# An encoder layer on one core: the mixing's output projection with all eight feature tiles by seven block products, in two sets

## The chip, the core and the metric

The kernel runs on one core of a Trainium2 chip. Time is device time in microseconds of one launch. The core has five engines with queues of their own: TensorE (PE), VectorE (DVE), ScalarE (ACT), GpSimd (POOL) and SyncE (SP). SP and POOL also issue most of the DMAs. Each engine works through its queue in order, and engines wait for each other on semaphores.

## What is computed

One encoder layer over 512 tokens with 1024 channels, in float32: a half-step feed-forward, a mixing of two attention branches, and a second half-step feed-forward, each with an RMS norm ahead and behind.

```python
f = _swiglu(_rmsnorm(x, ffn1_pre_g[l]), ffn1_w_gate[l], ffn1_w_up[l], ffn1_w_down[l])
x = x + 0.5 * _rmsnorm(f, ffn1_post_g[l])
h = _rmsnorm(x, mix_pre_g[l])
proj = h @ w_in[l]
...
ya = _neighbourhood_attention(...) @ w_branch_a[l]
yb = _dilated_mixture(qb, kb, vb, slopes) @ w_branch_b[l]
merged = jax.nn.sigmoid(gate_a) * ya + jax.nn.sigmoid(gate_b) * yb
x = x + _rmsnorm(merged @ w_out[l], mix_post_g[l])
f = _swiglu(_rmsnorm(x, ffn2_pre_g[l]), ffn2_w_gate[l], ffn2_w_up[l], ffn2_w_down[l])
x = x + 0.5 * _rmsnorm(f, ffn2_post_g[l])
```

The change is in `merged @ w_out`: 512 tokens, 1024 features in, 1024 out.

## The kernel before

**Precision.** Each float32 operand is split into a high part (rounded to fp32r, a copy by ScalarE) and a low part (what is left, a subtraction by VectorE), in `split`, lines 110 and 111. A product is three matmuls, high with high, high with low and low with high, in `mm3`, lines 189 to 191.

**Block products.** Much of the kernel multiplies 2 x 2 blocks by seven products in place of eight. In the output projection the tokens are in halves, the outputs in halves, and the features in pairs of tiles that make up the two halves of a set. The class `Blocks` holds this. A product number i (1 to 7) takes a token operand and a weight operand. Some are blocks and some are sums of blocks: `tokens` makes the token sums on VectorE (lines 615 and 620), the weight sums `t1` to `t4` are made by DMAs that add into SBUF (issued by POOL), and one, `t2`, by VectorE in `rows`. `prep` splits both operands of one product. `run` does its 12 matmuls: two row tiles of 128 tokens, two features, three matmuls each. The results add up in pairs of PSUM banks: `q` (products 1, 4, 6, 7), `r` (product 2), `c` (5 and 3) and, before the change, `z`. `onto` moves one pair onto another: ScalarE copies the bank to SBUF (`part`, line 672), VectorE adds it (line 678).

**The stage.** A loop over eight tiles f makes `merged`, tile by tile: 30 matmuls each, two gated products and a sum on VectorE (lines 1303 to 1313). Tiles 0 to 3 become the operands of the seven block products, and tiles 4 to 7 are kept as `hidden` and multiplied in the ordinary way by `one`, with four weight pieces of their own. The list `order` says in which order operands are prepared, `seq` in which order the first seven steps run. Beside these, `by_dma` loads the first four weight pieces of the second feed-forward: POOL issues the high loads (line 136), ScalarE writes the negated copy (line 139), and POOL issues a load that adds the original to it (line 141).

**The end of the stage.** `rows_out` walks over the four row tiles t (row 0 to row 3, 128 tokens each) and over the last steps of each. When a half of a row is complete, ScalarE takes its sum of squares (`junk`, line 248) and VectorE multiplies it by the gain (line 435). When both are, POOL makes the reciprocal root (lines 256 to 260) and VectorE the new `x` (line 475), whose squares ScalarE takes again. `pre_norm` then makes the normalised row (line 268), TensorE transposes it (line 277), and ScalarE and VectorE copy it out as `hn` (lines 280 and 281). Here `turn` says behind which step of row t the row before is normalised and the one before that is transposed. The second feed-forward begins in `first_pairs` with row tiles 0 and 1, at line 203, and does the transposes of rows 2 and 3 between its first products.

**What sets the order.** A scheduler orders the instructions by a timeline of its own, except where the kernel pins them: from `ordered.append([mark()])` on to the first products of the feed-forward, PE, ACT and DVE keep the order of the program text. POOL keeps it from `way_out` on, and SP through the first feed-forward. The pool `wp` has room for six split weight pieces of 128 x 1024, high and low, and the next split waits until the product that used the oldest has run. The pool `hp` has four rooms, `ra` to `rd`, of two raw pieces each.

Of the kernel before, what the change touches and what calls it, by code (L numbers as in the profile page):

```python
# [13 lines left out]
F32R = mybir.dt.float32r  # L14
BF16 = mybir.dt.bfloat16
AF = mybir.ActivationFunctionType
ALU = mybir.AluOpType
# [3 lines left out]
P = 128  # L21
T = 512
D = 1024
NK = D // P
# [6 lines left out]
NPIECE = 6  # L31
SPREAD = 4
URGENT = 400
FIRST = (4, 5, 6, 7)
STD = 3
BLOCKS = (10, 10)
BYDMA = (2, 3, 4)
# [6 lines left out]
def block_kernel(ctx, tc, x, gains, weights, rpb_near, rpb_all, alibi0, alibi12, out):  # L44
    nc = tc.nc
# [12 lines left out]
    def unit(dt=F32, name="u"):  # L58
        return up.tile([P, 512], dt, tag="u", name=name)
# [6 lines left out]
    def bank(name="ps"):  # L66
        return pp.tile([P, 512], F32, tag="ps", name=name)
# [33 lines left out]
    def gain(i):  # L101
        g = gp.tile([P, D], F32, tag="gain", name=f"gain{i}")
        nc.sync.dma_start(g, gains[i:i + 1, :].partition_broadcast(P))
        return g
# [4 lines left out]
    def split(hi, lo, src):  # L109
        nc.scalar.copy(hi, src)  # L110
        nc.vector.tensor_tensor(lo, src, hi.bitcast(F32), op=ALU.subtract)  # L111


    pieces = {}
# [47 lines left out]
    def cut(w, c, n):  # L162

        return [a[c // 512][:, c % 512:c % 512 + n] for a in w]

    def take(ahead=True):
        w = pieces.pop(state["take"])
        state["take"] += 1
        if ahead:
            fill(NPIECE - 1)  # L170
        return w
# [16 lines left out]
    def mm3(o, sh, sl, mh, ml, start, stop, **kw):  # L188
        nc.tensor.matmul(o, sh, mh, start=start, stop=False, **kw)  # L189
        nc.tensor.matmul(o, sh, ml, start=False, stop=False, **kw)  # L190
        nc.tensor.matmul(o, sl, mh, start=False, stop=stop, **kw)  # L191
# [364 lines left out]
    class Blocks:  # L556
# [38 lines left out]
            self.raw[key] = to  # L595
            nc.sync.dma_start(to, block(*kind, d))

        def load_sum(self, key, at, *of):

            to = self.raw[key, 0] = self.duo_room(*at)  # L600
            nc.sync.dma_start(to, self.block(*of[0], 0))
            for b in of[1:]:
                yield
                nc.gpsimd.dma_start(to, self.block(*b, 0), accum_op=ALU.add)
            yield

        def tokens(self, i, d):

# [479 lines left out]
    def mixing(g):  # L1088
# [106 lines left out]
        g_post, g_pre = gain(g), gain(g + 1)  # L1195
# [19 lines left out]
        seq = [(g, h) for g in (1, 2, 0) for h in range(4)]  # L1215
# [20 lines left out]
        step(len(pend))  # L1236


        hidden = [None] * 8
        parts = {}  # L1240
        duos = [[None] * 2 for _ in range(2)]
        n0 = total - 3 * NF - NK
        o = Blocks(n0, 1, duos)
        sub, add = ALU.subtract, ALU.add
        b00, b01, b10, b11 = (0, 0), (0, 1), (1, 0), (1, 1)
        sums = []
        way_out = mark()

        def stat(k):
            if k not in parts:  # L1250
                parts[k] = unit(F32R), unit(F32R)
                split(*parts[k], hidden[k])
                hidden[k] = None
            return parts[k]

        def load_rows(n):
            if n == 0:
                sums.extend([o.load_sum(b10, ("ra", 0), b10), o.load_sum(b00, ("ra", 1), b00),
                             o.load_sum("t1", ("rb", 0), b00, b01), o.load_sum("t2", ("rb", 1), b00, b01, b11),
                             o.load_sum("t3", ("rc", 0), b11, b01), o.load_sum(b11, ("rc", 1), b11),  # L1260
                             o.load_sum("t4", ("rd", 0), b00, b01, b11, b10)])
            for l in sums:
                next(l, None)

        wt = {}
        rooms = deque()

        def one(acc, t, k, first=False):

            w = wt[k]  # L1270
            for i in range(2):
                hh, hl = stat(k[0] + i)
                ts = slice(t * P, (t + 1) * P)
                mm3(acc, hh[:, ts], hl[:, ts], *cut(w, i * 512, 512), first and i == 0, i == 1, skip_group_check=True)

        order = [(2, 0), (1, 0), ("z", 4, 1), (5, 0), (6, 0), ("r", 4, 0), (7, 0), (3, 0), ("w", 6, 0), ("w", 6, 1), (4, 0)]
        seq = order[:7]
        ready = []

        def prep(n):  # L1280
            while len(ready) <= min(n, len(order) - 1):
                s = order[len(ready)]
                ready.append(s)
                if len(s) == 2:
                    o.prep(*s)
                else:
                    for i in range(2):
                        stat(s[1] + i)
                    i = n0 + 4 + len(wt)
                    convert(i, rooms.popleft() if rooms else None)  # L1290
                    wt[s[1:]] = pieces.pop(i)

        br = {}
        for f in range(8):
            ya, yb = bank(), bank()
            for k in range(10):
                i, c = divmod((f * 10 + k) * P, PIECE)
                if i not in br:
                    br[i] = take()
                mm3(ya if k < 4 else yb, *cut(br[i], c, P), o_parts[k][0], o_parts[k][1],  # L1300
                    k in (0, 4), k in (3, 9))
            m1, m2 = unit(), unit()
            nc.vector.tensor_tensor(m1, ya, sig[f], op=ALU.mult)
            nc.vector.tensor_tensor(m2, yb, sig[8 + f], op=ALU.mult)
            if f < 4:
                for i in range(2):
                    if f % 2 == 0:
                        duos[i][f // 2] = unit(name="h")
                    part = slice(i * 256, i * 256 + 256)
                    nc.vector.tensor_tensor(duos[i][f // 2][:, (f % 2) * 256:(f % 2) * 256 + 256],  # L1310
                                            m1[:, part], m2[:, part], op=ALU.add)
            else:
                nc.vector.tensor_tensor(m1, m1, m2, op=ALU.add)
                hidden[f] = m1
                stat(f)
            if 1 <= f <= 4:
                load_rows(f - 1)
            if f == 4:
                rooms.append(o.duo_room("rd", 1))
                nc.sync.dma_start(rooms[-1], weights[n0 + 4])  # L1320
            if f in FIRST:
                prep(FIRST.index(f))
                if f > 4:
                    o.prep_tokens(f, 0)
                    rooms.append(o.duo_room("ra", f - 5) if f < 7 else o.duo_room("rb", 0))
                    nc.sync.dma_start(rooms[-1], weights[n0 + f])
        state["take"] = state["next"] = n0 + 8
        state["stop"] = total - 3 * NF + 2 * STD

        whole[:] = [[unit(name="whole") for _ in range(2)] for _ in range(2)]  # L1330
        early = [by_dma(n) for n in first_of_next()] * 2
        ordered.append([mark()])
        after = {(1, 0): ("r", "q", add), (5, 0): ("z", "c", add), (6, 0): ("c", "q", sub), (7, 0): ("z", "q", sub)}
        for n, s in enumerate(seq):
            if len(s) == 2:
                o.run(*s)
            else:
                for key in s[0]:
                    first = o.open(key)
                    for t in range(2):  # L1340
                        one(o.acc[key][t], t + 2 * (key in "qz"), s[1:], first)
            if s in after:
                o.onto(*after[s])
            prep(n + len(FIRST))
            for _ in range((2, 2, 1, 1, 1, 1, 0)[n]):
                next(early.pop(0))
        state["used"] = True
        state["next"] += SPREAD
        acc = o.acc["r"] + o.acc["q"], o.acc["c"] + o.acc["z"]
        tail = [((6, 0), (4, 1), (6, 1), "b")] * 2 + [((6, 1), (4, 0), (6, 0), "b")] * 2  # L1350

        def last(t, k):
            k = tail[t][k]
            if k == "b":
                o.run(4 if t > 1 else 3, 0, (t % 2,))
            else:
                one(acc[k[1]][t], t, k)

        rows_out(acc, range(4), (None, 0, 1, 1), last, lambda t, b: (0, 3, 3, 0)[b + 2 * (t > 1)], g_post, 1.0, g_pre, False, None, False)
        pool.append((way_out, mark(), (mybir.EngineType.Pool,)))  # L1360


# [39 lines left out]
    g_pre = [bank("gain"), bank("gain")]  # L1402
# [81 lines left out]
    for n0, n1, engines in [(*o, PINNED) for o in ordered] + [(0, state["sp"], (mybir.EngineType.SP,)), *pool]:  # L1484
        last = {}
# [58 lines left out]

def _out_pieces(w):

    n = len(w) // 2
    rest = _moving_pieces(w[n:])
    return np.concatenate([_moving_pieces(w[:n]), rest[[2, 0, 1, 3]]])


def _down_pieces(w, blocks):
# [52 lines left out]
```

## Time and profile before

| | us |
|---|---|
| median of 3 runs | 1090.49 |
| the runs | 1091.98, 1090.48, 1090.49 |
| the profiled execution | 1090.01 |
| its span | 1088.2 |
| output projection: first matmul to the first of the second feed-forward | 704.83 to 748.03 |

The span is the time between the first and the last instruction on the engines; the rest of the execution lies around it. A row of a timeline gives start and duration in us, the engine, the line, the operation, the tile written and the tiles read, the shape, how many were merged (x2), and in brackets the idle time ahead of it with what ended it. A tile name without its number stands for all its buffers. A matmul's duration in the profile is its passage through the pipeline; what it takes of TensorE is the distance between starts.

### The profile page before, as it was taken

How to read it: one execution, taken by the hardware profiler on the slowest of the kernel's cores; microseconds unless marked ns; L12 is line 12 of the kernel's file. 1: busy time of each engine (PE TensorE's matmuls, PEld its weight loads, DVE VectorE, ACT ScalarE, POOL GpSimd, SP SyncE). 2: the span in 40 equal slices, each digit the busy share in tenths (PEclk: the TensorE clock that was granted, in tenths of full speed). 3: DMA queues.
4: the chain of work that ended last, by engine and by line, in shares of the span. 5: the costliest groups of instructions: out<-in, count | busy, mean ns of one | idle time of the engine just before them, and what ended most of it. 6: DMA issues, size and time to landing. Idle time of an engine off the chain costs nothing. (4 is left out here: it accounts for less than half of the span.)

```text
span 1088.2 us, 18567 instructions
## 1 busy us (share of the span) xinstructions
PE 1078.8 (99%) x6821; PEld 977.7 (90%) x6821; DVE 819.7 (75%) x1514; ACT 649.3 (60%) x1300; POOL 177.9 (16%) x248
## 2 busy tenths in 40 slices
PE   9999999999999999999999999999999999999997
PEld 7999999998888988888988888888999999998886
DVE  7887777777987679876467654766897777779974
ACT  6555555565584767767656651375565555566662
POOL 3121122012334000000000001133131111114101
PEclk9999999999999999999999999999999999999999
DMA  6899898468994453332232239564577776769932
GB/s 215 223 200 241 217 244 207 138 164 252 233 296 101 126 183 119 135 90 79 66 104 78 78 118 300 162 116 140 140 188 206 196 170 182 200 174 248 237 139 77
DMA packets 90973, 184.59 MB, mean 170 GB/s; under 512 B 23553, under 2 KB 26113, under 8 KB 90882
## 3 DMA queue, kind: packets, MB, share of 16 engines
q1 hardware_dynamic: 64720, 131.03, 35.8%
q0 software_dynamic: 23472, 51.91, 26.8%
q8 instruction: 53, 0.87, 0.3%
q10 hardware_dynamic: 2690, 0.46, 0.2%
q14 instruction: 38, 0.31, 0.1%
HBM read 178.34 MB, written 7.58 MB: 171 GB/s over the span
## 5 line engine op out<-in xcount | busy, mean ns | idle before, releaser
L111 DVE TENSOR_TENSOR w<-raw,w 128x512 fp32r<-128x512 f32 (+1 forms) x139 | 129.3, 931 | 87.6 <-ACT w L110 87.0
L189 PE MATMUL ps<-hn,w 128*128 128x512 f32 (+1 forms) x488 | 174.9, 358 | 0.0
L110 ACT CAST w<-raw 128x512 fp32r<-128x512 f32 (+1 forms) x139 | 113.5, 819 | 102.5 <-DMA raw<-in_weights_dram 41.5
L191 PE MATMUL ps<-hn,w 128*128 128x512 f32 (+1 forms) x488 | 172.4, 353 | 0.0
L190 PE MATMUL ps<-hn,w 128*128 128x512 f32 (+1 forms) x488 | 172.3, 353 | 0.0
L110 ACT CAST w<-t 128x512 fp32r<-128x512 f32 x152 | 93.5, 619 | 52.0 <-DVE t L334 27.9
L111 DVE TENSOR_TENSOR w<-t,w 128x512 fp32r<-128x512 f32 x152 | 103.9, 688 | 27.1 <-ACT w L110 24.4
L191 PEld LDWEIGHTS ps<-hn,w 128*128 128x128 f32 x488 | 92.3, 189 | 12.9
L190 PEld LDWEIGHTS ps<-hn,w 128*128 128x128 f32 x488 | 92.4, 189 | 11.3
L189 PEld LDWEIGHTS ps<-hn,w 128*128 128x128 f32 x488 | 92.4, 189 | 11.3
L189 PE MATMUL q<-v,w 128*128 128x256 f32 x304 | 86.0, 283 | 0.0
L191 PE MATMUL q<-hn,w 128*128 128x256 f32 x304 | 86.0, 283 | 0.0
L189 PE MATMUL p<-v,w 128*128 128x256 f32 x304 | 86.0, 283 | 0.0
L190 PE MATMUL p<-v,w 128*128 128x256 f32 x304 | 86.0, 283 | 0.0
L191 PE MATMUL q<-v,w 128*128 128x256 f32 x304 | 86.0, 283 | 0.0
L190 PE MATMUL q<-v,w 128*128 128x256 f32 x304 | 86.0, 283 | 0.0
L190 PE MATMUL q<-hn,w 128*128 128x256 f32 x304 | 86.0, 283 | 0.0
L189 PE MATMUL q<-hn,w 128*128 128x256 f32 x304 | 86.0, 283 | 0.0
L191 PE MATMUL p<-v,w 128*128 128x256 f32 x304 | 85.9, 283 | 0.0
L328 POOL DMA_DIRECT2D t<-in_weights_dram x38 | 33.3, 877 | 289.5 <-DMA t<-in_weights_dram 67.3
L189 PE MATMUL q<-w,a 128*128 128x512 f32 x176 | 68.5, 390 | 0.0
L190 PE MATMUL q<-w,a 128*128 128x512 f32 x176 | 68.3, 389 | 0.0
(260 smaller groups left out, 2992.6 us busy)
## 6 DMA issues: line engine op xcount, KB each, us to landing
raw<-in_weights_dram SPq DMA_DIRECT2D x103, 512.0 KB
t<-in_weights_dram SPq DMA_DIRECT2D x76, 256.0 KB
t<-in_weights_dram POOLq DMA_DIRECT2D x76, 256.0 KB, 5.3
w<-in_weights_dram SPq DMA_DIRECT2D x38, 256.0 KB
w<-in_weights_dram POOLq DMA_DIRECT2D x36, 256.0 KB, 6.3
rows<-in_weights_dram SPq DMA_DIRECT2D x24, 256.0 KB
tb<-in_weights_dram POOLq DMA_DIRECT2D x12, 512.0 KB, 7.9
x<-in_x_dram SPq DMA_DIRECT2D x16, 256.0 KB
```

What stands on the lines that cost most here:

```text
L110: nc.scalar.copy(hi, src)
L111: nc.vector.tensor_tensor(lo, src, hi.bitcast(F32), op=ALU.subtract)
L189: nc.tensor.matmul(o, sh, mh, start=start, stop=False, **kw)
L190: nc.tensor.matmul(o, sh, ml, start=False, stop=False, **kw)
L191: nc.tensor.matmul(o, sl, mh, start=False, stop=stop, **kw)
L328: nc.gpsimd.dma_start(t1, weights[n][:, :512], accum_op=ALU.add)
```

## The change

All eight tiles of `merged` become operands of seven block products, in two sets d = 0 and 1 (tiles are taken in the pairs 0, 2, 1, 3 of `TURNS`, and the matrix is laid out accordingly on the host). There are then 14 products, and no ordinary tile. The pair `z` is gone: the result of product 5 of both sets is copied from `c` to SBUF (`saved["c"]`), that of product 1 from `q` (`saved["q"]`). `r` gets the saved `q` added, and the saved `c` has the later `q` subtracted, which stands for what `z` was. The last product 7 is divided: its row tile for rows 0 and 2 runs in the loop, that for rows 1 and 3 at the start of row 2 in `rows_out`. There are now three steps per row: rows 0 and 1 have three of 6 matmuls each, row 2 has three and row 3 has two.

```diff
-FIRST = (4, 5, 6, 7)
+TURNS = (0, 2, 1, 3)
+EARLY = (2, 2, 0, 0, 0, 1, 1, 1, 1)
...
-        o = Blocks(n0, 1, duos)
+        o = Blocks(n0, 2, duos)
...
+        def load_rows(f):
+            if f == 1:
+                sums.extend([o.load_sum((b00, d), ("ra", d), b00) for d in range(2)] +
+                            [o.load_sum(("t1", d), ("rb", d), b00, b01) for d in range(2)])
+            elif f == 2:
+                sums.extend([o.load_sum(("t3", d), ("rc", d), b11, b01) for d in range(2)] +
+                            [o.load_sum((b10, d), ("rd", d), b10) for d in range(2)])
...
+        def first_rows(f):
+
+            if f == 4:
+                o.prep(1, 0)
+                o.prep_tokens(5, 0)
+            elif f == 5:
+                o.prep(1, 1)
+                o.load((b11, 0), "ra", 0)
...
+            elif f == 6:
+                o.prep(5, 0)
+                o.load((b11, 1), "ra", 1)
+                o.load(("t2", 0))
...
+            elif f == 7:
+                o.prep(5, 1)
+                o.load(("t2", 1))
...
+        seq = [(i, d) for i in (1, 5, 6) for d in range(2)] + [(2, 0), (7, 0), (7, 1)]
+        order = [(2, 0), (7, 0), (7, 1), (2, 1), (3, 0), None, (3, 1), (4, 0), (4, 1)]
+        for d in range(2):
+            o.prep(6, d)
+            o.load(("t4", d))
+        saved = {}
         for n, s in enumerate(seq):
...
+            o.run(*s, *[(0,)] * (s == (7, 1)))
+            if s in ((1, 1), (5, 1)):
+                key = "q" if s[0] == 1 else "c"
+                saved[key] = [o.part(key, t) for t in range(2)]
+            elif s == (6, 1):
+                o.onto("c", "q", sub)
+            elif s == (2, 0):
+                for t in range(2):
+                    nc.vector.tensor_tensor(o.acc["r"][t], o.acc["r"][t], saved["q"][t], op=add)
+            elif s == (7, 1):
+                nc.vector.tensor_tensor(saved["c"][0], saved["c"][0], o.acc["q"][0], op=sub)
+            if order[n]:
+                o.prep(*order[n])
+            for _ in range(EARLY[n]):
                 next(early.pop(0))
...
-        tail = [((6, 0), (4, 1), (6, 1), "b")] * 2 + [((6, 1), (4, 0), (6, 0), "b")] * 2
...
         def last(t, k):
...
+            if t < 2:
+                o.run(*((2, 1), (3, 0), (3, 1))[k], (t,))
+            elif k + t == 2:
+                o.run(7, 1, (1,))
+                nc.vector.tensor_tensor(saved["c"][1], saved["c"][1], o.acc["q"][1], op=sub)
+            elif k + t < 5:
+                o.run(4, k + t - 3, (t - 2,))
...
-        rows_out(acc, range(4), (None, 0, 1, 1), last, lambda t, b: (0, 3, 3, 0)[b + 2 * (t > 1)], g_post, 1.0, g_pre, False, None, False)
+        rows_out((o.acc["r"] + o.acc["q"], o.acc["c"] + saved["c"]), range(3), (None, 0, 1, 0), last,
+                 lambda t, b: ((0, 2), (0, 2), (2, None), (1, 0))[t][b], g_post, 1.0, g_pre, False, None, False)
```

The lines of the changed kernel are shifted: line 110 of before is 111 there, 139 is 140, 248 is 249, 268 is 269, 280 is 281, 475 is 476. How the instructions stand on the engines, at two places:

ScalarE from the last copy of `q` to the first sums of squares of the row tiles, in the kernel before (`w` is a split weight set or a piece for the next stage, `a` a token split, `ssf` the sums of squares):

```order
L672 COPY part<-q 128x512 x2
L110 CAST a<-h 128x512
L110 CAST w<-rd 128x1024
L248 ACTIVATE junk,ssf<-r 128x512
L248 ACTIVATE junk,ssf<-c 128x512
```

The same place on ScalarE in the changed kernel, behind the last copy of `q`:

```order
L140 ACTIVATE w<-w 128x512 x2
L111 CAST a<-v 128x512
L111 CAST w<-ra 128x1024
L140 ACTIVATE w<-w 128x512 x2
L111 CAST a<-h 128x512
L111 CAST w<-rb 128x1024
L140 ACTIVATE w<-w 128x512 x2
L111 CAST a<-h 128x512
L111 CAST w<-rb 128x1024
L140 ACTIVATE w<-w 128x512 x2
L249 ACTIVATE junk,ssf<-part 128x512
L249 ACTIVATE junk,ssf<-r 128x512
```

Between the last copy and the sums there were two operations, now there are fourteen, and a sum over `part` is new. The negated copies stood ahead of that last copy before.

VectorE in the changed kernel at the same time (L1320 is the addition of the saved `q` to `r`, `v` a token sum):

```order
L678 TENSOR_TENSOR c<-c,part 128x512 x2
L1320 TENSOR_TENSOR r<-r,part 128x512 x2
L620 TENSOR_TENSOR v<-v,h 128x512
L112 TENSOR_TENSOR a<-v,a 128x512
L112 TENSOR_TENSOR w<-ra,w 128x1024
```

The last token sum `v`, and with it ScalarE's `a<-v` above, now stands behind the additions to `r`, which need product 2 of the first set.

VectorE around the end of row 1, in the kernel before (`hn` is the copy of a transposed row tile, `u` a weighted or normalised half row):

```order
L435 TENSOR_TENSOR u<-c,gain_5026 128x512
L475 SCALAR_TENSOR_TENSOR x<-u,rstd,x 128x512 x2
L435 TENSOR_TENSOR u<-z,gain_5026 128x512
L281 TENSOR_TENSOR hn<-ps,hn 128x4x128 x2
L268 SCALAR_TENSOR_TENSOR u<-x,rstd,gain_5028 128x512 x2
```

And in the changed kernel:

```order
L436 TENSOR_TENSOR u<-c,gain_5026 128x512
L476 SCALAR_TENSOR_TENSOR x<-u,rstd,x 128x512 x2
L1336 TENSOR_TENSOR part<-part,q 128x512
L282 TENSOR_TENSOR hn<-ps,hn 128x4x128 x2
L269 SCALAR_TENSOR_TENSOR u<-x,rstd,gain_5028 128x512 x2
```

The subtraction of the second `q` bank from the saved `c` (L1336), behind which TensorE may write that bank again, stands behind the new `x` of row 1.

More of the change, by code (lines that the diff above doesn't have):

```diff
@@ L596, in load, with load_sum @@
             nc.sync.dma_start(to, block(*kind, d))
[L598 to L604, printed above, removed]
+        def load_sum(self, key, at, of, *more):
+            to = self.raw[key] = self.duo_room(*at)
+            nc.sync.dma_start(to, self.block(*of, key[1]))
             yield
+            for b in more:
+                nc.gpsimd.dma_start(to, self.block(*b, key[1]), accum_op=ALU.add)
         def tokens(self, i, d):
@@ L1236, in mixing @@
         step(len(pend))
-        hidden = [None] * 8
-        parts = {}
-        duos = [[None] * 2 for _ in range(2)]
+        duos = [[None] * 4 for _ in range(2)]
         n0 = total - 3 * NF - NK
-        o = Blocks(n0, 1, duos)
+        o = Blocks(n0, 2, duos)
         sub, add = ALU.subtract, ALU.add
@@ L1247, in mixing @@
         way_out = mark()
[L1249 to L1261, printed above, removed]
+        def load_rows(f):
[5 more added lines that the diff above has]
+                            [o.load_sum((b10, d), ("rd", d), b10) for d in range(2)])
@@ L1262, in load_rows @@
             for l in sums:
                 next(l, None)
[L1265 to L1291, printed above, removed]
+        def first_rows(f):
[5 more added lines that the diff above has]
+                o.load((b11, 0), "ra", 0)
+                o.prep_tokens(6, 0)
+                o.prep_tokens(2, 0)
+            elif f == 6:
+                o.prep(5, 0)
+                o.load((b11, 1), "ra", 1)
+                o.load(("t2", 0))
+                o.prep_tokens(7, 0)
+                o.prep_tokens(3, 0)
+            elif f == 7:
+                o.prep(5, 1)
+                o.load(("t2", 1))
@@ L1304, in mixing @@
             nc.vector.tensor_tensor(m2, yb, sig[8 + f], op=ALU.mult)
[L1305 to L1326, printed above, removed]
+            at = TURNS[f // 2]
+            for i in range(2):
+                if f % 2 == 0:
+                    duos[i][at] = unit(name="h")
+                part = slice(i * 256, i * 256 + 256)
+                nc.vector.tensor_tensor(duos[i][at][:, (f % 2) * 256:(f % 2) * 256 + 256],
+                                        m1[:, part], m2[:, part], op=ALU.add)
+            if 1 <= f <= 3:
+                load_rows(f)
+            first_rows(f)
         state["take"] = state["next"] = n0 + 8
@@ L1332, in mixing @@
         ordered.append([mark()])
-        after = {(1, 0): ("r", "q", add), (5, 0): ("z", "c", add), (6, 0): ("c", "q", sub), (7, 0): ("z", "q", sub)}
-        for n, s in enumerate(seq):
[L1335 to L1345, printed above, removed]
+        seq = [(i, d) for i in (1, 5, 6) for d in range(2)] + [(2, 0), (7, 0), (7, 1)]
[4 more added lines that the diff above has]
+        saved = {}
+        for n, s in enumerate(seq):
+            o.run(*s, *[(0,)] * (s == (7, 1)))
[12 more added lines that the diff above has]
+            for _ in range(EARLY[n]):
                 next(early.pop(0))
@@ L1348, in mixing @@
         state["next"] += SPREAD
-        acc = o.acc["r"] + o.acc["q"], o.acc["c"] + o.acc["z"]
-        tail = [((6, 0), (4, 1), (6, 1), "b")] * 2 + [((6, 1), (4, 0), (6, 0), "b")] * 2
         def last(t, k):
[L1353 to L1357, printed above, removed]
-        rows_out(acc, range(4), (None, 0, 1, 1), last, lambda t, b: (0, 3, 3, 0)[b + 2 * (t > 1)], g_post, 1.0, g_pre, False, None, False)
+            if t < 2:
[7 more added lines that the diff above has]
+                 lambda t, b: ((0, 2), (0, 2), (2, None), (1, 0))[t][b], g_post, 1.0, g_pre, False, None, False)
         pool.append((way_out, mark(), (mybir.EngineType.Pool,)))
@@ L1545, in _out_pieces @@
 def _out_pieces(w):
-    n = len(w) // 2
-    rest = _moving_pieces(w[n:])
-    return np.concatenate([_moving_pieces(w[:n]), rest[[2, 0, 1, 3]]])
+    return _moving_pieces(w.reshape(4, 2 * P, -1)[list(TURNS)].reshape(NK * P, -1))
 def _down_pieces(w, blocks):
```

## Prediction, made before the changed kernel had run

> **What bounds the kernel now.** I read the page first, then the waits of TensorE alone, then the busy time of each engine in the stretch that the change rewrites, and last that stretch instruction by instruction.
>
> ```profile
> span 1088.2 us, 18567 instructions
> PE 1078.8 (99%) x6821; PEld 977.7 (90%) x6821; DVE 819.7 (75%) x1514; ACT 649.3 (60%) x1300; POOL 177.9 (16%) x248
> PE ps L203 <- ACT hn L280: 0.4, 1, 0.4
> 720.00:730.00 10.00, 10.00 (x45) 8.23 (x44) 8.14 (x10) 8.82 (x16) 5.90 (x7) 1.00 0.82 120
> ```
>
> The last row's columns are the stretch, its length, then PE, weight loads, VectorE, ScalarE and GpSimd with their instructions, the granted clock, the DMAs' share and GB/s. TensorE (PE) is busy 99% of the span, and its only wait inside the stages is 0.4 us, on the copy of `hn` that opens the second feed-forward. So a matmul that goes is worth its full slot, but only while the other engines still deliver in time. In 720 to 730 us, the end of the stretch, ScalarE (ACT) is busy 8.82 us of 10 and VectorE (DVE) 8.14: there is little room for more work at this place.
>
> ```profile
> 704.83 0.39 PE L189 MATMUL r<-w,a 128*128 128x512 f32 x1
> ...
> 729.12 0.39 PE L191 MATMUL c<-w,a 128*128 128x512 f32 x1
> ...
> 737.28 0.39 PE L191 MATMUL q<-w,u 128*128 128x512 f32 x1
> 737.52 1.03 PE L277 MATMUL ps<-ident,u 128*128 128x128 f32 x8
> 738.31 0.48 PE L189 MATMUL q<-w,u 128*128 128x512 f32 x1
> ...
> 748.03 1.22 PE L203 MATMUL ps<-hn,w 128*128 128x256 f32 x8 [0.40 <-ACT hn L280]
> ...
> 751.00 1.04 PE L277 MATMUL ps<-ident,u 128*128 128x128 f32 x8
> ```
>
> The output projection runs from 704.83 to 748.03. Between the first row and that of 737.28 lie 143 matmuls, so one takes 0.2269 us. A group of eight transposes takes 0.79, and the matmul behind it starts 0.08 late.
>
> **What it saves on TensorE.** Before: 84 matmuls of seven block products and 96 of four ordinary feature tiles, 180. After: 14 products of 12, 168. Twelve fewer are 12 x 0.2269 = 2.72 us. Without any wait the new stage ends at 704.83 + 168 x 0.2269 + 2 x 0.87 = 744.69, which is 3.34 before 748.03 (the 2.72 and the old wait with its start).
>
> **What it adds on ScalarE and VectorE, and where.** Fourteen weight sets are split in place of eleven, and the tokens give fourteen splits and eight sums in place of eleven and four. What counts is the place. The rows of the order show that three sets, three token tiles and three pairs of scaled copies (L139) now stand on ScalarE between the addition to `r` and the first row sum. These are its rows:
>
> ```profile
> 717.85 0.62 ACT L110 CAST a<-v 128x512 fp32r<-128x512 f32 x1 [1.36 <-DVE v L620]
> 718.38 1.05 ACT L110 CAST w<-rc 128x1024 fp32r<-128x1024 f32 x1
> 719.33 1.15 ACT L139 ACTIVATE w<-w 128x512 fp32r<-128x512 f32 x2
> 720.38 1.05 ACT L672 COPY part<-q 128x512 f32<-128x512 f32 x2
> ...
> 726.26 0.64 ACT L110 CAST a<-h 128x512 fp32r<-128x512 f32 x1
> 726.78 1.06 ACT L110 CAST w<-rd 128x1024 fp32r<-128x1024 f32 x1
> 727.73 0.61 ACT L248 ACTIVATE junk<-r 128x512 bf16<-128x512 f32 x1
> 729.61 0.60 ACT L248 ACTIVATE junk<-c 128x512 bf16<-128x512 f32 x1 [1.18 <-PE c L191]
> 732.28 0.63 ACT L248 ACTIVATE junk<-x 128x512 bf16<-128x512 f32 x1 [1.98 <-DVE x L475]
> ...
> 733.79 0.60 ACT L248 ACTIVATE junk<-r 128x512 bf16<-128x512 f32 x1
> ...
> 738.21 0.63 ACT L248 ACTIVATE junk<-x 128x512 bf16<-128x512 f32 x1 [2.47 <-DVE x L475]
> ...
> 740.35 1.07 ACT L280 CAST hn<-ps 128x512 fp32r<-128x512 f32 x2
> ...
> 745.25 0.63 ACT L248 ACTIVATE junk<-x 128x512 bf16<-128x512 f32 x1 [3.18 <-DVE x L475]
> ...
> 746.81 0.60 ACT L248 ACTIVATE junk<-z 128x512 bf16<-128x512 f32 x1
> 747.40 1.07 ACT L280 CAST hn<-ps 128x512 fp32r<-128x512 f32 x2
> ```
>
> From start to start, a token split costs ScalarE 0.52 (726.26 to 726.78), a weight set 0.95, a pair of L139 1.05, two sums of squares 1.51 (732.28 to 733.79). Those of VectorE:
>
> ```profile
> 712.03 1.23 DVE L111 TENSOR_TENSOR w<-ra,w 128x1024 fp32r<-128x1024 f32 x1 [0.24 <-ACT w L110]
> ...
> 717.13 0.68 DVE L620 TENSOR_TENSOR v<-v,h 128x512 f32<-128x512 f32 x1
> ...
> 731.44 1.41 DVE L475 SCALAR_TENSOR_TENSOR x<-u,rstd,x 128x512 f32<-128x512 f32 x2 [0.41 <-POOL rstd L260]
> 734.51 0.69 DVE L435 TENSOR_TENSOR u<-r,gain 128x512 f32<-128x512 f32 x1 [1.66 <-ACT junk L248]
> 735.12 1.41 DVE L268 SCALAR_TENSOR_TENSOR u<-x,rstd,gain 128x512 f32<-128x512 f32 x2
> 736.44 0.68 DVE L435 TENSOR_TENSOR u<-c,gain 128x512 f32<-128x512 f32 x1
> 737.36 1.41 DVE L475 SCALAR_TENSOR_TENSOR x<-u,rstd,x 128x512 f32<-128x512 f32 x2 [0.24 <-POOL rstd L260]
> ...
> 742.29 1.41 DVE L268 SCALAR_TENSOR_TENSOR u<-x,rstd,gain 128x512 f32<-128x512 f32 x2
> 744.41 1.41 DVE L475 SCALAR_TENSOR_TENSOR x<-u,rstd,x 128x512 f32<-128x512 f32 x2
> ```
>
> Up to there the work fits. Between 704.83 and 724.15 VectorE has six weight sets (at 1.23), four token splits, three token sums and five other additions of a bank or of branch tile 7 (at about 0.69 each): 7.4 + 8.3 = 15.7 us of 19.3. No step of TensorE is late in that stretch by this count.
>
> Then step by step. The set `r` is complete after 84 matmuls, 723.89. In the rows, ScalarE starts on a bank 0.26 after its last slot (729.12 plus 0.23, to 729.61); so the second addition to `r` starts at 724.15. It holds VectorE's queue: behind it stands the token sum `v` of the last set (0.61 later, 724.76), and ScalarE's split `a<-v` follows that by 0.72 (717.13 to 717.85): 725.48. ScalarE then works without a pause: 3 x (0.52 + 0.95 + 1.05) = 7.56, so its first sum of squares, of `part`, starts at 733.04, that of `r` at 733.80, that of `c` at **734.55**. Row 0 was complete on TensorE after 120 matmuls, 732.06. In the kernel before, the sum of `c` came 0.26 behind the product; now it comes 2.2 later than that.
>
> From here I carry on by distances of the same pairs of rows.
> - Row 0 (the first 128 tokens): `c` to `x` 1.83, `x` to its squares 0.84, those two 1.51 (738.73), to the normalised row (L268) 1.33: 740.06. Its halves are done at 740.76 and 741.47. TensorE's plan has the transposes at 738.87 to 739.66 (after 150 matmuls); with four transposes taking 0.40 they end at 741.87. **Wait 2.2.**
> - Row 1: `x` 2.00 after L268 (2.24 in the rows less the 0.24 of waiting), 742.06. Behind this pair (1.32) stands VectorE's new subtraction of `q` from the kept `c`, 743.38 to 744.08; TensorE may write that bank of `q` only then, and is there at 743.31. **Wait 0.8.**
> - The `hn` copies of row 0 come 0.85 + 1.51 after `x`: 744.42. L268 of row 1 comes 1.8 later (1.94 in the rows, 740.35 to 742.29, less 0.15 for an operation that has moved): 746.22. Halves at 746.92 and 747.63; transposes end at 748.03, planned 746.23. **Wait 1.8.**
> - Row 2: `x` 2.12 after that L268, 748.34; squares 0.84 later; those two and that of `part` 1.56 + 0.59; so the `hn` copies of row 1 start at 751.33 and the second feed-forward 0.63 later, at **751.96**. TensorE's last matmul of the stage ends at 749.5. **Wait 2.5.**
>
> Why that last chain bites: before, row 1 had 48 matmuls behind it, now 30, so 4.1 us of cover are gone, whatever ScalarE does. Sum: 2.2 + 0.8 + 1.8 + 2.5 = 7.3 of waits, less 3.34: **+3.9 us**.
>
> Costs at nothing: the block order of the matrix in memory (made on the host), TensorE's matmuls in the rest of the kernel (the same rows in both orders), rows 2 and 3 (their distances to the start of the feed-forward stay as they were, and their transposes had 0.7 us to spare or more). The sum of squares and the product with the gain now read SBUF for `part`: between the rows for `x` (0.63) and for a bank (0.60), so 0 to 0.1 us. The unknown is the sums that the DMAs make:
>
> ```profile
> w<-in_weights_dram POOLq DMA_DIRECT2D x36, 256.0 KB, 6.3
> tb<-in_weights_dram POOLq DMA_DIRECT2D x12, 512.0 KB, 7.9
> ...
> rc<-in_weights_dram POOLq DMA_DIRECT2D x1, 512.0 KB, 14.9
> ```
>
> ```profile
> 700.30 4.28 POOL L136 DMA_DIRECT2D w<-in_weights_dram  x8 [16.76 <-PE ps L191]
> ```
>
> The sum `t2` now lands between two splits of the same buffer. With 7.9 us it is there when VectorE comes to it; with 14.9 it would be 7 late. I take 7.9: the DMAs have little else to do then, since seven sums by POOL early in the stage become four. Of the same queue: the eight loads of L136 for the next stage now stand behind the four later sums, the last of which waits for the split of the sixth set, about 712 by the counts above. The loads then take 4.28, to 717, and land 6.3 after their issue, the first pair near 720 and the last near 723.5; L139 wants them from 721.9 to 731.9. So I cost this at nothing; up to 2 us later it would still hide in ScalarE's pause before 725.5.
>
> **Rivals.**
> - *All hidden*: ScalarE's queue is short and the chains fit; the gain stays whole, -3.3. For it: 99% on PE. Against: the distances above. 0.09. [...] The trace's 8.82 of 10 on ScalarE at this place speaks against it.
> - *ScalarE in time, tail too short*: the sum of `c` at 732.32. Then no wait at the first transposes, but L268 of row 1 at 743.72, `hn` of row 1 at 748.83 and the feed-forward at 749.46: +1.4, so 1091.9. It needs the nine operations to be done 2.2 us sooner. 0.14.
> - *The DMA sums land late*, 14.9: VectorE's 3.6 us of slack take half, the rest moves the whole tail by 2.5 to 7, say 4.5: +8.4, 1098.9. 0.05.
> - *TensorE's clock falls in the waits.* It was granted in full (1.00 in the window row), and the wait there was 0.4 us. With four waits in 13 us it could fall; the first 2.97 us of the feed-forward (748.03 to 751.00) at half pace would be 3.0 more: 1097.4. 0.05. [...]
>
> **How the numbers follow.** The profiled execution took 1090.01 us, its span of 1088.2 and 1.8 around it, which the change does not touch; +3.9 is 1093.9. The median of the runs shown, 1090.49, is 0.48 above it: **1094.4**. My forecast has 0.67. The range 1091.5 to 1096.8 takes in the forecast within 2.5 and the second rival, 0.81 together. Slower by over 0.2% (2.2 us, about what a measurement can tell) is most of the forecast and the last two rivals, 0.72; within, the second rival and the forecast's low edge, 0.19; faster, 0.09.
>
> **What would show it.** Right: TensorE with waits of 0.5 to 3 us ahead of both groups of transposes and ahead of L203's matmuls in the new profile, ScalarE without a gap for some 7.5 us up to the squares of `part`, and those of the first `c` over 2 us behind its last matmul. Wrong: those squares within 0.5 us of the product, or a wait of TensorE before `r` is complete, which would point to the DMAs.

## The result and the profile after

| | before | after |
|---|---|---|
| median of 5 runs, us | 1090.49 | 1095.36 |
| lowest and highest | 1090.43, 1093.62 | 1093.52, 1095.70 |
| the profiled execution, its span | 1090.01, 1088.2 | 1095.36, 1093.6 |

The ratio of the times is 1.0035, with a 95% interval of 1.0023 to 1.0046, so the changed kernel is slower by 2.5 to 5.0 us. The two profiled executions lie 5.35 apart, a little more than that interval, since the one of before was among the fastest of its kernel and that of after had one of the two lowest mean clocks of its five (0.995). They serve below for where the time went, the ratios for how much it is. Of the changed kernel's lines named below, L204 is the old L203 and L278 the old L277.

The head of the new page, then TensorE's waits inside the stages (engine, tile and line, what it waited for, us, times, longest):

```profile
span 1093.6 us, 18557 instructions
PE 1080.4 (99%) x6809; PEld 977.7 (89%) x6809; DVE 828.8 (76%) x1526; ACT 653.2 (60%) x1304; POOL 179.1 (16%) x249
```

```profile
PE ps L204 <- ACT hn L281: 2.3, 1, 2.3
PE ps L278 <- DVE u L269: 2.1, 2, 1.8
```

Twelve matmuls fewer (6809 for 6821), yet TensorE is busy 1.6 us longer, and it waits 4.4 us where it waited 0.4. That a matmul takes longer there is seen in the table of stretches (stretch, length, PE, weight loads, VectorE, ScalarE, GpSimd, then the granted clock):

```profile
735.00:740.00 5.00, 4.17 (x19) 3.13 (x17) 2.85 (x5) 2.88 (x9) 2.04 (x7) 1.00 1.08 227
740.00:745.00 5.00, 4.04 (x16) 3.10 (x17) 4.18 (x8) 2.28 (x8) 2.24 (x6) 0.73 0.35 131
745.00:750.00 5.00, 4.32 (x20) 2.86 (x18) 4.90 (x8) 1.85 (x6) 2.59 (x5) 0.93 0.06 20
750.00:755.00 5.00, 3.13 (x17) 3.13 (x18) 3.38 (x6) 2.81 (x8) 3.12 (x6) 0.75 0.25 92
```

The clock, 1.00 before the waits, is 0.73 and 0.75 in two of the stretches behind them. TensorE's timeline of the changed kernel shows both waits and what follows them:

```profile
705.01 0.39 PE L190 MATMUL q<-w,a 128*128 128x512 f32 x1
...
738.79 0.39 PE L192 MATMUL q<-w,a 128*128 128x512 f32 x1
740.95 1.32 PE L278 MATMUL ps<-ident,u 128*128 128x128 f32 x8 [1.77 <-DVE u L269]
742.03 0.57 PE L190 MATMUL q<-w,a 128*128 128x512 f32 x1
...
745.39 0.53 PE L192 MATMUL q<-w,a 128*128 128x512 f32 x1
...
746.90 1.32 PE L278 MATMUL ps<-ident,u 128*128 128x128 f32 x8 [0.29 <-DVE u L269]
...
751.87 1.58 PE L204 MATMUL ps<-hn,w 128*128 128x256 f32 x8 [2.26 <-ACT hn L281]
...
756.34 0.93 PE L278 MATMUL ps<-ident,u 128*128 128x128 f32 x7
```

Nine matmuls from 742.03 to 745.39 include eight steps of 0.42 on the average, against 0.227 before the wait. The stage begins 0.18 later than before (705.01 for 704.83). The second feed-forward starts 46.86 after that first matmul; before it was 43.20: **3.66** more. And its first products, up to the next transposes, take 4.47 in place of 2.97: **1.50** more, at the lower clock. 0.18 + 3.66 + 1.50 = 5.34 is the difference of the spans, 5.4. The next transposes after those stand 5.35 later than before (762.97 for 757.62), so nothing more is lost behind them.

ScalarE's timeline, at the place where the prediction saw the delay:

```profile
725.58 0.62 ACT L111 CAST a<-v 128x512 fp32r<-128x512 f32 x1 [2.41 <-DVE v L620]
...
732.08 1.15 ACT L140 ACTIVATE w<-w 128x512 fp32r<-128x512 f32 x2
733.13 0.62 ACT L249 ACTIVATE junk<-part 128x512 bf16<-128x512 f32 x1
...
734.59 0.60 ACT L249 ACTIVATE junk<-c 128x512 bf16<-128x512 f32 x1
```

From 725.58 to 733.13 no row has an idle time in brackets: 7.55 us of splits and scaled copies ahead of the first sum of squares, and behind a pause of 2.41 in which ScalarE had waited for `v`. The squares of the first `c` come 29.58 after the stage's first matmul; before, 24.78.

### The profile page after: what moved, and what is told of

Read it like the earlier page. It is cut to its first block, busy times and chain, and to the rows that moved or that the text cites. A ratio compares the mean times of both kernels' runs of the same rounds, so it can differ in the third digit from the quotient of the medians.

```text
span 1093.6 us, 18557 instructions
## 1 busy us (share of the span) xinstructions
PE 1080.4 (99%) x6809; PEld 977.7 (89%) x6809; DVE 828.8 (76%) x1526; ACT 653.2 (60%) x1304; POOL 179.1 (16%) x249
## 5 line engine op out<-in xcount | busy, mean ns | idle before, releaser
L190 PE MATMUL q<-w,a 128*128 128x512 f32 x192 | 75.5, 394 | 0.0
L191 PE MATMUL q<-w,a 128*128 128x512 f32 x192 | 75.3, 393 | 0.0
```

## The experiments

Each profile was laid on the stage's first matmul, since executions reach it up to 3.2 us apart. Times in the text are in us. The columns are: the squares of row 0's `c` on ScalarE and the start of the second feed-forward, both counted from there; the first products of that feed-forward (up to its first transposes); and the time as a ratio to runs of the kernel before on the same chip.

| kernel | squares of c | feed-forward | first products | ratio, 95% interval |
|---|---|---|---|---|
| before | 24.78 | 43.20 | 2.97 | 1 |
| after | 29.58 | 46.86 | 4.47 | 1.0035 (1.0023 to 1.0046) |
| early | 28.02 | 45.41 | 4.33 | 1.0025 (1.0016 to 1.0034) |
| late2 | 30.87 | 48.43 | 4.44 | 1.0052 (1.0039 to 1.0065) |
| fill | 29.58 | 46.96 | 2.95 | 1.0028 (1.0016 to 1.0039) |
| early_fill | 28.02 | 45.71 | 2.95 | 1.0016 (1.0007 to 1.0025) |
| early_r | 27.57 | 44.97 | 4.43 | 1.0021 (1.0012 to 1.0030) |
| skip4 | 27.46 | 44.74 | 4.47 | 1.0023 (1.0013 to 1.0033) |
| skip4_fill | 27.46 | 45.72 | 2.95 | 1.0025 (1.0016 to 1.0035) |
| before_late | 27.56 | 45.67 | 2.98 | 1.0017 (1.0008 to 1.0026) |
| before_later | 30.79 | 49.16 | 2.96 | 1.0066 (1.0052 to 1.0080) |
| tail3 | 22.19 | 51.01 | 2.87 | 1.0067 (1.0054 to 1.0079) |
| tail4 | 25.38 | 48.90 | 2.87 | 1.0055 (1.0043 to 1.0068) |
| tail5 | 29.54 | 52.49 | 2.87 | 1.0136 (1.0119 to 1.0153) |

My theory was that of the prediction: ScalarE's queue starts row 0's chain late, and the tail has less cover; with it the fall of the clock, which the new trace had shown. The rivals were the tail alone, the clock alone, or nothing of ScalarE's.

**early: ScalarE's queue shorter.** Three of the four pairs of scaled copies go into ScalarE's pause ahead of `v`.

```diff
-EARLY = (2, 2, 0, 0, 0, 1, 1, 1, 1)
+EARLY = (2, 2, 0, 0, 0, 3, 1, 0, 0)
```

> Three of the four pairs of ScalarE copies that stand in its queue between the copy of v and the copies of the tail (three groups of some 3 us each with the one that stays) are moved into its pause ahead of the copy of v. My theory (ScalarE's queue ends 2.2 us late, so the tail's two chains start late): junk c ends near 732.6 instead of 734.59, the transposes of row 0 start without a wait, the feed-forward starts near 749.7 instead of 751.87, and the time falls by 2 to 3.6 us to 1091.7 to 1093.3 (the larger end if the TensorE clock then also stays at full pace in the feed-forward's first products). Rival, the tail has too few matmuls whatever ScalarE does: feed-forward start within 0.5 us of 751.87, time 1095.0 to 1095.7. Rival, the lower clock alone: start unchanged, time unchanged.

The squares of `c` came 1.56 earlier, the feed-forward 1.45, not 2.2; the ratio fell from 1.0035 to 1.0025, 1.1 us, with intervals that overlap. So the direction is that of my theory and the size is not. The reason stands on VectorE's timeline of this kernel: no pause from the last split to row 0's `x`, where the changed kernel still waits 0.55 and 0.41 (in front of 734.59 and 736.41 there).

```profile
732.39 1.22 DVE L112 TENSOR_TENSOR w<-rb,w 128x1024 fp32r<-128x1024 f32 x1
733.52 0.69 DVE L436 TENSOR_TENSOR u<-part,gain 128x512 f32<-128x512 f32 x1
734.13 0.68 DVE L436 TENSOR_TENSOR u<-r,gain 128x512 f32<-128x512 f32 x1
734.73 0.68 DVE L436 TENSOR_TENSOR u<-c,gain 128x512 f32<-128x512 f32 x1
735.33 1.40 DVE L476 SCALAR_TENSOR_TENSOR x<-u,rstd,x 128x512 f32<-128x512 f32 x2
```

VectorE, which the prediction had followed only up to the completion of `r`, is the next to be late.

**late2: ScalarE's queue longer.**

```diff
+        for _ in range(2):
+            nc.scalar.copy(sp.tile([P, 512], BF16, tag="junk", name="junk", bufs=1), saved["c"][1])
         rows_out(...
```

> Two ScalarE copies of 128x512 are added ahead of the first sums of squares (extra work, output unaffected), some 1.1 us together. My theory (ScalarE sets the start of the two chains): feed-forward start 1.0 to 1.1 us later, near 752.9, time 1096.4. Rival, VectorE or the matmuls of the tail set it: start and time unchanged within 0.3 us.

The two copies took 1.29 of ScalarE (1.1 was my estimate), and the feed-forward came 1.57 later. The start follows ScalarE one for one and a little more; the rival (unchanged) is out.

**early_r: VectorE relieved too, on top of early.**

```diff
 elif s == (2, 0):
-    for t in range(2):
-        nc.vector.tensor_tensor(o.acc["r"][t], o.acc["r"][t], saved["q"][t], op=add)
+    at = o.tokens(3, 1)
+    o.a[3, 1] = unit(F32R, "a"), unit(F32R, "a")
+    nc.vector.tensor_tensor(o.acc["r"][0], o.acc["r"][0], saved["q"][0], op=add)
+    split(*o.a[3, 1], at)
+    nc.vector.tensor_tensor(o.acc["r"][1], o.acc["r"][1], saved["q"][1], op=add)
```

> The kernel with the three moved pairs of ScalarE copies, and in it the two additions to r on VectorE no longer stand ahead of v and its split: the order becomes v, addition of row 0, split of v, addition of row 1. My theory after the run with the moved pairs (with ScalarE's queue shortened, VectorE's queue is the next to hold the tail: it works without pause up to row 0's x): w of the next product is complete about 0.8 us earlier, x of row 0 and the feed-forward start 0.6 to 0.9 us earlier than in the run with the moved pairs (735.33 and 750.77 there), so near 750.0, and the time 0.6 to 0.9 us lower, near 1093.5. Rival, ScalarE's copies of the tail or the 24 matmuls hold row 0: x of row 0 and the time unchanged within 0.3 us.

`c` and the feed-forward came 0.45 and 0.44 earlier than in early. That is above the 0.3 of the rival and below the 0.6 to 0.9 that I expected. In time (1.0021 after 1.0025) it can't be told from no change.

**skip4: neither engine late.** On top of early, product 4 takes over the splits of product 3; its own are left out, and with them its part of the output.

```diff
 def prep(self, i, d):
+    if i == 4 and self.nd == 2:
+        self.a[i, d], self.w[i, d] = self.a[3, d], self.w[3, d]
+        return
```

> The kernel with the three moved pairs of ScalarE copies, and product 4 uses the token and weight splits of product 3 (its own two token splits and two weight splits are left out, so its part of the output is not computed; TensorE's work is the same). ScalarE and VectorE are then free before row 0 is complete on TensorE. This is the second rival of the prediction by itself (ScalarE in time, only the tail's cover too short). My theory: row 0's squares of c follow their product (732.3 to 732.6 on the time scale of the changed kernel's profile), feed-forward start 749.4 to 750.0 there, that is 1.9 to 2.4 us earlier than 751.87, and its first products still at half pace if the wait ahead of it is near 2 us: time 2.0 to 3.4 below the changed kernel, 0.4 to 1.9 above the kernel before. Rival, the queues cost little and the short cover everything: feed-forward start within 0.8 us of 751.87 and time 3 us or more above the kernel before. Rival, the queues cost everything: time 2 us or more below the kernel before.

ScalarE's timeline here shows a wait for the product itself:

```profile
730.32 0.60 ACT L249 ACTIVATE junk<-r 128x512 bf16<-128x512 f32 x1
...
732.99 0.60 ACT L249 ACTIVATE junk<-c 128x512 bf16<-128x512 f32 x1 [1.98 <-PE c L192]
```

And TensorE's:

```profile
732.50 0.39 PE L192 MATMUL c<-w,a 128*128 128x512 f32 x1
```

The last matmul of row 0 started at 732.50, its slot ends at 732.73, and the squares follow 0.26 later, as in the kernel before. This is the second rival of the prediction, made real. The feed-forward starts at 44.74, still 1.54 later than before, and 2.12 earlier than in the changed kernel. So of the 3.66, 2.12 are late queues, and 1.54 stay without them. By early, which takes the pairs away alone, 1.56 of the 2.12 at `c` are in those pairs, and by early_r 0.45 in VectorE's order; 0.11 is left for the splits. In time the ratio of 1.0023 is 2.5 us, above the 0.4 to 1.9 that I had given; the first products were at the lower clock again (0.66 from 750 to 755).

The 1.54 is read from distances in the table. Row 0 is complete after 120 matmuls, where it was complete after 108, so the squares of its `c` come 2.68 later than before (27.46 for 24.78). From there to the feed-forward it is 17.28, in the changed kernel as in skip4 (17.39 to 17.56 in early, early_r and late2), and 18.42 in the kernel before. So row 0's chain takes nearly the same time in each, and the matmuls behind row 0, now 48 in place of 72, are its cover: the work of TensorE beside which it runs unseen. That more cover would win the 1.54 back is argued and not shown.

**fill, early_fill, skip4_fill: the clock.** TensorE transposes the identity into banks that are about to be overwritten while it would wait.

```diff
+        for _ in range(state.pop("first", 0)):
+            nc.tensor.transpose(ps[0][:, :P], ident, ident)
...
+        for _ in range(state.get("fill", [0] * 9).pop(0) if state.get("fill") else 0):
+            nc.tensor.transpose(pt[:, :P], ident, ident)
...
+        state["fill"], state["first"] = [17, 4, 7, 4], 22
```

> Idle TensorE is given transposes of the identity into PSUM banks that are about to be overwritten, ahead of the transposes of the four row chunks and ahead of the feed-forward's first products, so that it works through its waits (extra work, output unaffected). If the waits bring the clock down (my reading of the trace): granted clock 1.00 in the stretch 740 to 760, feed-forward start still near 751.9, its first products in 3.0 us instead of 4.5, time 1.5 us lower, near 1093.9. Rival, the clock falls for another reason: clock still 0.73 to 0.93 there, time unchanged. Rival, the extra transposes delay the real ones: time 1096 to 1097.

> The moved pairs and the filling transposes together. If the two losses are apart (start of the feed-forward 1.1 us earlier by the moved pairs; clock drop of 1.5 us removed, with 0.4 us given back, by the filling): granted clock 1.00 from 740 to 760, feed-forward start 751.0 to 751.3, time near 1093.3. Rival, they overlap (the filling delays the now earlier transposes): feed-forward start 751.6 or later, time 1094 or more.

> The same with the filling transposes that keep TensorE at work in its waits (product 4's own splits left out here too). If the lower clock adds 1.5 us behind a wait of about 2 us: the feed-forward starts as in the run without filling (within 0.4 us), its first products take 3.0 us instead of 4.5, time 0.7 to 1.5 us lower than that run. Rival: time unchanged within 0.4 us.

The rows of fill's stretches:

```profile
740.00:745.00 5.00, 4.73 (x33) 3.93 (x32) 4.43 (x7) 2.28 (x7) 2.24 (x6) 1.00 0.36 130
745.00:750.00 5.00, 4.65 (x30) 3.85 (x30) 4.65 (x8) 1.89 (x6) 2.72 (x5) 1.00 0.08 32
750.00:755.00 5.00, 5.00 (x45) 5.00 (x44) 3.37 (x6) 3.12 (x10) 3.02 (x6) 1.00 0.30 110
```

The clock stays at 1.00, and the first products take 2.95 with the start unchanged (46.96 for 46.86). So the waits do bring the clock down, and that costs 1.5 in the trace; in time 1.0028 after 1.0035 is 0.8, within the intervals. Together with the moved pairs (early_fill) the feed-forward starts 0.30 later than in early and the ratio is 1.0016, the lowest of the change's own order, though its interval overlaps that of early. In skip4_fill the 22 transposes were too many for a shorter wait: they moved the start by 0.98, which gave back most of the 1.52, and the time didn't fall. It tells nothing against the clock.

**before_late and before_later: the same chain in the kernel before.** Six copies of 128x512 on ScalarE ahead of its first sum of squares, and `range(11)` in the second.

```diff
+        for _ in range(6):
+            nc.scalar.copy(sp.tile([P, 512], BF16, tag="junk", name="junk", bufs=1), o.duos[0][0])
         rows_out(acc, range(4), (None, 0, 1, 1), last, ...
```

> The kernel before, with six ScalarE copies of 128x512 (3.2 to 3.4 us) ahead of the first sums of squares (extra work, output unaffected); its ScalarE had 1.2 us to spare there. My theory (the rows' chain sets the feed-forward's start in both kernels, the number of matmuls matters only as cover): row 0's squares of c 2.0 to 2.2 us later than 729.61, feed-forward start 1.0 to 2.2 us later than 748.03, and the first products of the feed-forward at a lower clock if the wait ahead of it passes 2 us: time 1.0 to 3.7 us above the kernel before. Rival, the 24 matmuls of each row cover it: feed-forward start within 0.4 us of 748.03, time unchanged.

> The kernel before with eleven ScalarE copies of 128x512 (7.1 us by the 0.65 of the run with six) ahead of the first sums of squares, extra work, output unaffected. Row 0's squares of c then come some 6.0 us later than 729.61. My theory: waits of 4 us or more ahead of the first transposes, so the clock falls here too, in a kernel without the change; feed-forward start 5 to 6 us late, time 5 to 8 us above the kernel before. Rival, the clock's fall belongs to the changed kernel: clock 1.00 in all windows from 735 to 760, time 5 to 6 us above.

With six, `c` came 2.78 later (more than foretold, as a copy took 0.65) and the feed-forward 2.47; with eleven 6.01 and 5.96. So 24 matmuls a row cover next to nothing of a later row 0: the chain over ScalarE and VectorE sets the end in this kernel as well (18.11 and 18.37 from `c` to the feed-forward), and in the kernel before it was just in time. With six, TensorE's waits were 1.06 and 0.86, and the clock stayed at 1.00. With eleven the first wait was 4.26, and the matmuls behind it ran at 0.43 each. That run's stretch there (now TensorE alone, the clock, the DMAs' share and GB/s):

```profile
745.00:750.00 5.00, 4.99 (x19) 0.66 0.28 105
```

So the fall belongs to no one kernel. Here it had recovered by the feed-forward (1.00 from 750 to 760).

**tail3, tail4, tail5: trying for a version that is faster than both.** If row 0's chain sets the end, row 0 should be complete sooner. In these the loop runs products 1, 5 and 6 alone; then each row tile has 24 matmuls as in the kernel before, and row 0 is complete after 96 matmuls, not 120. The diffs show the main lines only.

```diff
-seq = [(i, d) for i in (1, 5, 6) for d in range(2)] + [(2, 0), (7, 0), (7, 1)]
+seq = [(i, d) for i in (1, 5, 6) for d in range(2)]
...
+    o.run(*((2, 0), (2, 1), (3, 0), (3, 1))[k], (t,))
...
+    o.run(*((7, 0), (7, 1), (4, 0), (4, 1))[k], (t - 2,))
```

> The seven products are put in another order: in the loop products 1, 5 and 6 of both sets, after it products 2 and 3 for the first two row chunks and 7 and 4 for the other two, so that a row chunk has 24 matmuls in the tail as in the kernel before, and row 0 is complete after 96 matmuls instead of 120; two pairs of ScalarE copies and the preparation of the last weights stand in ScalarE's pauses of the tail. My theory (the time from row 0's end to the feed-forward is a chain of 18.7 us over ScalarE and VectorE as soon as row 0's end comes in time): row 0 ends near 726.6, feed-forward start 745.3 to 746.5, time 1087.8 to 1089.5, faster than both. Rival, ScalarE still has too much ahead of row 0's end or in the rows: feed-forward start 748 to 750, time 1090.5 to 1093. Rival, the weights' preparation comes late for TensorE: waits ahead of the first matmuls of product 7 or 4, time 1092 or more.

tail4 against tail3 (the list of turns and the place of the pauses' work change too):

```diff
+    if n in (2, 3):
+        o.prep_tokens((7, 4)[n - 2], 1)
...
-state["gaps"] = {0: lambda: o.prep(7, 1), 1: lambda: o.prep(4, 1), ...
+state["gaps"] = {0: lambda: o.prep(4, 1), 1: lambda: next(early.pop(0)), 2: lambda: next(early.pop(0))}
...
+    if (t, k) == (0, 2):
+        o.prep(7, 1)
```

> The other order of products with 24 matmuls in every row chunk, its weights' preparation moved: product 7's second set is prepared ahead of row 0's squares of c, product 4's behind row 0's squares of x, their tokens earlier still, and two pairs of ScalarE copies stand behind the squares of x of rows 1 and 2. My theory: row 0's squares of c near 727.9, x of row 0 near 730, no wait over 1 us for the additions or subtractions, feed-forward start 745.5 to 747.2, time 1087.8 to 1090. Rival, VectorE cannot take the preparation inside the rows' chain: feed-forward start 748 to 750, time 1090.5 to 1094.

tail5 against tail4 (`pool` holds for the second sets of products 7 and 4, and one token difference and the place of product 4's preparation change too):

```diff
-def split(hi, lo, src):
+def split(hi, lo, src, pool=False):
     nc.scalar.copy(hi, src)
-    nc.vector.tensor_tensor(lo, src, hi.bitcast(F32), op=ALU.subtract)
+    (nc.gpsimd if pool else nc.vector).tensor_tensor(lo, src, hi.bitcast(F32), op=ALU.subtract)
```

> The order with 24 matmuls in every row chunk, row 0 complete after 96 matmuls, and the subtractions of the last two preparations (second sets of products 7 and 4: one difference of tokens, two splits of tokens, two splits of weights) on GpSimd, which has little to do there, in place of VectorE; product 4's weights are prepared behind row 0's rstd, three pairs of ScalarE copies behind the squares of x of rows 1 to 3. My theory (VectorE's and ScalarE's queues, not TensorE, hold the tail; with VectorE freed of 5.3 us the start follows the matmuls): row 0's squares of c near 728 to 728.5, x of row 0 near 730, feed-forward start 745.5 to 747.5, no wait of TensorE over 1.5 us ahead of it, time 1088 to 1090.5, 0 to 2.5 us below the kernel before. Rival, GpSimd is too slow (1.28 us for a 128x512 subtraction elsewhere in the trace) and holds product 7 or the rstd of row 0: waits of TensorE on the split weights, time 1092 to 1097.

All three were slower. In tail3 `c` did come at 22.19, 2.59 sooner than before. But product 4 adds into the bank `q` that product 7 has filled, and VectorE's subtraction of that bank stood in its queue behind row 1's `x` and two splits. TensorE's timeline of tail3:

```profile
744.41 0.79 PE L190 MATMUL q<-w,a 128*128 128x512 f32 x1 [6.41 <-DVE part L1347]
```

In tail4 the preparation was moved ahead of that, and VectorE came to the subtraction of `q` from `c` too late for product 3. Its timeline of TensorE:

```profile
730.28 0.50 PE L190 MATMUL c<-w,a 128*128 128x512 f32 x1 [3.07 <-DVE c L686]
```

So the work of the last two preparations had no room on VectorE at either of the places that I tried, in the rows' chain and ahead of it. tail5 gave its subtractions to GpSimd, and that made VectorE itself slower. First VectorE's timeline, then GpSimd's:

```profile
714.93 1.22 DVE L112 TENSOR_TENSOR w<-rd,w 128x1024 fp32r<-128x1024 f32 x1
716.23 1.85 DVE L112 TENSOR_TENSOR a<-h,a 128x512 fp32r<-128x512 f32 x1
...
727.67 3.43 DVE L112 TENSOR_TENSOR w<-rb,w 128x512 fp32r<-128x512 f32 x2
...
738.89 3.48 DVE L477 SCALAR_TENSOR_TENSOR x<-u,rstd,x 128x512 f32<-128x512 f32 x2 [0.41 <-POOL rstd L261]
```

```profile
715.89 1.62 POOL L620 TENSOR_TENSOR v<-h 128x512 f32<-128x512 f32 x1
...
728.09 2.46 POOL L112 TENSOR_TENSOR w<-rc,w 128x1024 fp32r<-128x1024 f32 x1 [0.89 <-ACT w L111]
...
738.84 2.99 POOL L112 TENSOR_TENSOR w<-rb,w 128x512 fp32r<-128x512 f32 x2
```

Every slow row of VectorE overlaps one of GpSimd: 1.85 for 0.69, 3.43 for 1.29, 3.48 for 1.41. Each of the three ends 0.54 to 0.57 behind GpSimd's. TensorE then waited 5.03 for `c`. No version that I ran is faster than the kernel before.

## Why the prediction was right, step by step

- *The saving, 3.34.* Right. TensorE works without a wait up to its last matmul ahead of the first transposes, whose slot ends at 739.02 (738.79 and 0.23); the plan had 738.87, and the stage began 0.18 later.
- *No lateness until `r` is complete, the DMA sums among it.* Right: TensorE's waits have no other entry in the stage, and `v`, the end of that count, starts on VectorE at 724.86 for the 724.76 foretold.
- *ScalarE without a pause for 7.56, `c` at 734.55.* Right: 7.55, 734.59. The runs early, late2 and skip4 show that it is the cause of part of the loss and not only beside it. That ScalarE alone holds it was my reading; with its queue cut (early), 0.56 of the 2.12 was left, and 0.45 of that was VectorE's order.
- *Row 0.* The normalised row at 740.15 (740.06 foretold), the wait 1.77 (2.2).
- *Row 1.* `x` 742.08 (742.06), the subtraction 743.41 (743.38), `hn` of row 0 744.30 (744.42), the normalised row 746.10 (746.22). The waits of 0.8 and 1.8 did not appear as such, there is one of 0.29: TensorE, at a clock of 0.50 just then (0.42 a matmul), came late itself. Its slower matmuls took the place of the waits, so here the clock cost little.
- *Row 2 and the feed-forward.* `hn` of row 1 at 751.25 (751.33), the start at 751.87 (751.96), the wait 2.26 (2.5).
- *The sum.* +3.9 was foretold. Measured in the traces, 3.66 from the first matmul of the stage to the feed-forward. The prediction's split of it, 1.4 with ScalarE in time and 2.5 by the queues, is 1.54 and 2.12 by skip4.
- *The clock.* This is what the sum lacked: a rival with 0.05, at 3.0. It came, at 1.50, because half pace (a granted clock of 0.50) lasted only from 752.50 to 755.91, 3.41, and not for all of the first products. The prediction had waits of up to 2.5 and still gave the fall 0.05: waits of 1.77 and 2.26 were enough. With it the sum would have been 1095.4 on the profile's scale, where the profiled execution took 1095.36. By the ratio, 3.8 over 1090.49 is 1094.3, so the medians cannot tell which of the two sums is nearer. That the forecast of 1094.4 lies so near is in part luck: the profiled execution lost 3.66 and, through a term that the sum lacked, 1.50 more. The clock is also not the same in every execution: of the five of the changed kernel, two have a mean granted clock of 0.995, at 1095.36 (the profiled one) and 1095.70, and two have 0.998, at 1093.52 and 1094.81.
- *All hidden*, and *the DMA sums late*: neither happened.

## What to carry to other kernels

A matmul that is removed is a gain only as far as the engines behind it can follow: look at the last 20 us of the stage, count what stands in each queue ahead of the first operation of the chain that closes it, and do so for every engine on that chain, since the next one may be late by nearly as much. Work that is taken from TensorE's tail is also cover that is taken from that chain. And a wait can cost more than itself: in the changed kernel the first products behind the wait of 2.26 took 1.50 longer at the lower clock, while in tail5 the clock stayed at 1.00 behind one of 2.01.

## What the runs showed of the hardware

*The clock after short waits.* The granted clock of after, read in slices of 0.1 us from 725 to 765, is 1.00 or 0.50 but for the four slices with a change in them. It is 0.50 from 742.26 to 745.67 and from 752.50 to 755.91, 3.41 us each. The first of these begins 1.31 behind the end of the wait of 1.77 (740.95), the second 0.63 behind that of 2.26 (751.87). For the other runs the mean clock in stretches of 5 us shows the falls:

| run | stretches | clock |
|---|---|---|
| early, early_r, skip4 | 750 to 755 | 0.66 |
| late2 | 740 to 745, 745 to 750 | 0.92, 0.74 |
| late2 | 750 to 755, 755 to 760 | 0.94, 0.72 |
| before_later, tail4 | 745 to 750 | 0.66 |
| tail3 | 740 to 745, 745 to 750, 750 to 755 | 0.54, 0.50, 0.94 |
| tail5 | 735 to 740 | 0.85 |

A fall followed single waits of 1.77 and 2.26 (after), 2.27 (early, skip4), 2.26 (early_r), 3.07 and 2.54 (late2), 4.26 (before_later) and 1.86 (tail4, ahead of 745.43). In tail3 it began within the wait of 6.41; in tail5 the matmuls behind the wait of 5.03 took 0.43 each from the second on, up to 736.19. None followed 0.40 (before), 0.86 and 1.06 (before_late), 1.11 (early), 1.86 and 2.01 (tail5, ahead of 748.54 and 757.16), nor 3.07 in tail4, where the stretch that begins just ahead of the first matmul behind the wait (TensorE alone again) has a clock of 1.00:

```profile
730.00:733.00 3.00, 2.72 (x12) 1.00 0.59 83
```

So the length of a wait does not decide alone: 1.86 has a fall behind it in tail4 and none in tail5. What else decides was not shown, and no run was made to test it.

*VectorE beside GpSimd.* In the rows of tail5 above, three operations of VectorE took 2.5 to 2.7 times as long beside a subtraction or addition on GpSimd as without one (1.85 for 0.69, 3.43 for 1.29, 3.48 for 1.41). They ended 0.54 to 0.57 behind GpSimd's, which took 1.62, 2.46 and 2.99. Why was not shown.
